# Moving one row per partition from the last block to the first: 113 and 15 rows in place of 112 and 16, in a streaming row maximum

## The chip, the cores and the metric

The kernel runs on one core of one Trainium2 chip. The metric is device time in microseconds (us), lower is better. It is taken as the median of several runs of the whole program; a profiled execution of the same program gives the trace that is read below.

## The reference

The computation is the maximum over the last axis of a float32 array:

```python
def setup_inputs():
    batch, seq, dim = 32, 512, 1024
    return {"x": np.random.randn(batch, seq, dim).astype(np.float32)}

def reference(x):
    return np.max(x, axis=-1).astype(np.float32)
```

That is 16,384 rows of 1,024 numbers, 67.1 MB in, 64 KB out. Every number is read once, so the work is one long stream of loads with a reduction behind it.

## The kernel before

**Tiling.** The rows are spread over 128 partitions, so each partition has 128 rows of 4 KB. A "row" below means one row in every partition: 128 x 1,024 numbers, 512 KB. The 128 rows form two blocks (`BLOCKS`, lines 13 to 16). In the first block partition p holds the 112 consecutive rows of x that begin at row 112 p, in the second the 16 consecutive rows that begin at row 14,336 + 16 p. So the distance in memory between the data of neighbouring partitions is 112 rows (448 KiB) in the first block and 16 rows (64 KiB) in the second.

**Loads.** Each entry of `BLOCKS` is one load, issued on the sync engine's queue (SP), line 238, in the order of the list: loads 0 to 10 for the first block, 11 to 17 for the second. The last two rows of the second block are not in the list: they come as four pieces of less than a row each (`PIECES`, line 243). The loads land in a ring of 47 row slots in the on-chip memory (`RING`). A load that doesn't fit before the end of the ring starts again at slot 0 (lines 112 and 113). Loads 0 to 3 take slots 0 to 46, loads 4 to 7 slots 0 to 41, and loads 8 to 17 and the pieces go round once more: load 10 (7 rows) is in slots 16 to 22, loads 11, 12 and 13 (3 rows each) in 23 to 31, load 14 (2 rows) in 32 and 33, loads 15, 16 and 17 (one row each) in 34 to 36, the pieces from 37 on. A load is issued when every earlier load whose slots it overwrites has been read (`issue`, lines 231 to 244).

**Reductions.** The vector engine (DVE) does nearly all of the maximum, with one instruction for each load: step `dJ` of `PLAN` (lines 31 to 34) is `direct(J)`, which reduces all rows of load J that are not shared. Every instruction of the body comes from the helper `maximum`, line 78.

**Shared rows.** Four of the late loads share some of their rows with other engines (`SHARED`, line 20; an entry is load: (rows, column blocks of 128)). `10: (3, 8)` says that three of load 10's seven rows go whole (all eight column blocks) to the other engines, so `d10` is left with four rows. `13: (2, 3)`, `14: (2, 3)` and `17: (1, 2)` say that of two rows, two rows and one row the first 3, 3 and 2 column blocks go to the other engines, and the rest of these rows, 640, 640 and 768 numbers wide, is reduced on DVE by the steps `p13`, `p14` and `p17` (`partial`). Load 13 has three rows, so one is left for `d13`; load 14 has two rows, both shared, so there is no `d14`.

The other engines' path is a step `tK` (`turn`): TensorE (PE) transposes each 128 x 128 block into PSUM, ScalarE (ACT) copies the result to a buffer, GpSimd (POOL) takes the maximum over the partitions. A step `bK` (`back`) then brings the row of maxima back into columns with small PE transposes. A chunk is at most as many rows as fit eight column blocks: `t0`, `t1`, `t2` are the three rows of load 10 (1,024 columns each), `t3` the two rows of load 13 (768 columns), `t4` those of load 14 (768), `t5` that of load 17 (256). `m10` (a DVE maximum over the 3 x 8 numbers that came back) closes load 10's rows, `m99` (over the 5 shared rows of loads 13, 14 and 17) closes the others and is the last reduction of the kernel.

**Order.** `PLAN` is the order of the steps, written out by hand, and the instructions of each engine are tied to it (`in_turn`). On DVE it gives d0 to d10, d11, d12, d13, p13, p14, m10, d15, d16, p17, then the four pieces f0 to f3, then m99. No instruction of DVE can overtake another that still waits for its load. `RANK` (line 22) puts the shared rows of loads 13, 14 and 17 at the end of the block's columns, so that `m99` writes neighbouring columns.

**Stores.** The first block's results are stored once f0 is done (line 265), the second block's after m99 (line 267), both on ACT's queue.

Of the kernel before, what the change touches and what calls it, by code (L numbers as in the profile page):

```python
# [10 lines left out]


BLOCKS = [
    [2, 15, 16, 14, 11, 11, 10, 10, 8, 8, 7],
    [3, 3, 3, 2, 1, 1, 1],
]
RING = 47


SHARED = {10: (3, 8), 13: (2, 3), 14: (2, 3), 17: (1, 2)}  # L20

RANK = {13: 1, 14: 2, 17: 2}

# [17 lines left out]
def kernel(  # L41
# [76 lines left out]
    assert first == I  # L118
    shared = [SHARED.get(j, (0, C)) for j in range(len(loads))]

# [176 lines left out]
```

## Time and profile before

| | |
|---|---|
| median of 3 runs | 163.84 us (163.82 to 163.93) |
| span of the profiled execution, first to last instruction | 162.1 us |
| instructions | 295 |
| DVE busy | 135.3 us, of it 129.9 us in reductions from the ring to the result |
| POOL busy | 15.9 us |
| PE busy | 13.6 us |
| ACT busy | 6.3 us |
| read from memory | 67.11 MB, mean 414 GB/s over the span |
| DVE's waits for loads | 23.5 us in four pieces: 3.14, 15.85, 3.20 and 1.30 us |
| last reduction (m99) | from 159.66 us, 0.17 us |
| last store issued | 159.86 us, lands 1.4 us later |

The span leaves out what lies before the first and after the last instruction: the median is 1.74 us longer than the span of the profiled execution. A difference between two kernels inside the span carries over to the median.

Times in the timeline are microseconds from the span's start. The duration of a DVE instruction overlaps the next one's start by some 0.08 us, because the instructions are pipelined; where instructions follow each other without a wait, the distance from start to start is therefore the cost, and it is a little less than the duration. A DMA's line gives the time from its issue to its landing, so the landing is the start of the issuing instruction plus that time.

### The profile page before, as it was taken

The page shows a single profiled execution, that of the slowest core. Times are in us where ns is not written, and L with a number is a line of the kernel's source. Part 1 is how long each engine was busy: PE and PEld are TensorE (multiplying, and loading weights), DVE is VectorE, ACT ScalarE, POOL GpSimd, SP SyncE. Part 2 cuts the span into 40 slices and gives each one's busy share as a digit, 9 for nine tenths or more (in the row PEclk, how much of TensorE's full clock was granted, in tenths as well). Part 3 has the DMA queues.
Part 4 walks back from the last instruction along what each step waited for, and adds up shares of the span by engine and source line. Part 5 has one row for each costly group of instructions (what it writes and reads, how often), then busy time and mean ns, then how long its engine had stood idle before and what let it go on. Part 6 is the DMA issues. An engine that isn't in the chain of part 4 may idle for free.

```text
span 162.1 us, 295 instructions
## 1 busy us (share of the span) xinstructions
PE 13.6 (8%) x76; PEld 11.7 (7%) x76; DVE 135.3 (83%) x33; ACT 6.3 (4%) x7; POOL 15.9 (10%) x10
## 2 busy tenths in 40 slices
PE   0000000000000000000000000000000000772942
PEld 0000000000000000000000000000000000762731
DVE  3500019998399999999999999996999999999994
ACT  3000000000000000000000000000000000241120
POOL 0000000000000000000000000000000000099791
PEclk9999999999999999999999999999999999996555
DMA  5995999599879999898999799799999989999991
GB/s 178 566 485 258 470 501 517 259 517 517 354 340 439 453 404 534 356 523 367 478 411 475 334 485 475 334 485 388 477 429 388 466 382 446 415 421 416 411 388 34
DMA packets 3456, 67.18 MB, mean 414 GB/s; under 512 B 640, under 2 KB 896, under 8 KB 1536
## 3 DMA queue, kind: packets, MB, share of 16 engines
q1 hardware_dynamic: 3168, 67.11, 96.8%
q10 hardware_dynamic: 288, 0.07, 0.2%
HBM read 67.11 MB, written 0.07 MB: 414 GB/s over the span
## 4 chain that ended last, share of the span: by engine, by line
DMA 50%; DVE 47%; SPq 1%; issue 0%; DVEq 0%
DMA ring<-in_x_dram 50%; DVE ring L78 45%; DVE joint L78 2%; SPq L238 1%; DVEq L292 0%
## 5 line engine op out<-in xcount | busy, mean ns | idle before, releaser
L78 DVE TENSOR_REDUCE ring<-ring 128x1 f32<-128x1024 f32 (+13 forms) x20 | 129.9, 6547 | 23.5 <-DMA ring<-in_x_dram 23.5
L168 POOL PARTITION_ALL_REDUCE top<-sb x6 | 15.7, 2658 | 142.6 <-ACT sb L166 142.5
L160 PE MATMUL ps<-ident,ring 128*128 128x128 f32 x38 | 9.0, 423 | 140.0 <-DMA ring<-in_x_dram 140.0
L160 PEld LDWEIGHTS ps<-ident,ring 128*128 128x128 f32 x38 | 7.6, 225 | 140.1 <-issue 140.1
L166 ACT COPY sb<-ps 128x1024 f32<-128x1024 f32 (+2 forms) x6 | 5.0, 834 | 150.5 <-PE ps L160 143.5
L78 DVE TENSOR_REDUCE joint<-ring 128x2 f32<-128x1280 f32 (+1 forms) x3 | 3.9, 1314 | 0.0
L178 PE MATMUL got<-ident,top 1*128 1x1 f32 x24 | 2.7, 228 | 3.8 <-POOL top L168 3.6
L178 PEld LDWEIGHTS got<-ident,top 1*128 1x128 f32 x24 | 2.4, 188 | 4.6 <-POOL top L168 4.6
L178 PE MATMUL joint<-ident,top 1*128 1x1 f32 x14 | 2.0, 244 | 1.9 <-POOL top L168 1.9
L178 PEld LDWEIGHTS joint<-ident,top 1*128 1x128 f32 x14 | 1.7, 210 | 2.7 <-POOL top L168 2.7
L166 ACT ACT_TABLE_LOAD x1 | 1.3, 1283 | 0.7 <-PEq L281 0.7
L83 DVE MEMSET ident<- 128x128 f32 x1 | 0.2, 165 | 0.8 <-PEq L281 0.8
L90 DVE TENSOR_SCALAR rowno<-rowno 32x1 f32<-32x1 f32 x3 | 0.4, 146 | 0.1
L85 DVE TENSOR_TENSOR_SCAN colno<-ident 128x128 f32<-128x128 f32 x1 | 0.4, 425 | 0.0
L92 DVE TENSOR_SCALAR ident<-colno,rowno 128x128 f32<-128x128 f32 x1 | 0.3, 288 | 0.0
L87 DVE STREAM_TRANSPOSE rowno<-colno 128x32 f32<-128x32 f32 x1 | 0.2, 211 | 0.0
L78 DVE TENSOR_REDUCE ring<-got 128x3 f32<-128x24 f32 x1 | 0.2, 172 | 0.0
L78 DVE TENSOR_REDUCE ring<-joint 128x5 f32<-128x20 f32 x1 | 0.2, 170 | 0.0
L281 POOL MEMSET const-float32-0.0<- 128x1 f32 x1 | 0.1, 98 | 0.2 <-issue 0.2
L281 POOL MEMSET const-bfloat16-1.0<- 128x1 bf16 x1 | 0.1, 102 | 0.0
L281 POOL MEMSET const-uint8-127<- 128x1 uint8 x1 | 0.1, 101 | 0.0
L281 POOL MEMSET const-float32-1.0<- 128x1 f32 x1 | 0.1, 98 | 0.0
(1 smaller groups left out, 0.1 us busy)
## 6 DMA issues: line engine op xcount, KB each, us to landing
ring<-in_x_dram SPq DMA_DIRECT2D x2, 5632.0 KB, 29.9
ring<-in_x_dram SPq DMA_DIRECT2D x2, 5120.0 KB, 36.8
ring<-in_x_dram SPq DMA_DIRECT2D x2, 4096.0 KB, 32.5
ring<-in_x_dram SPq DMA_DIRECT2D x1, 7680.0 KB, 22.6
ring<-in_x_dram SPq DMA_DIRECT2D x1, 7168.0 KB, 58.0
ring<-in_x_dram SPq DMA_DIRECT2D x3, 1536.0 KB, 35.7
ring<-in_x_dram SPq DMA_DIRECT2D x1, 3584.0 KB, 29.2
ring<-in_x_dram SPq DMA_DIRECT2D x2, 1024.0 KB, 17.8
```

The lines of the kernel that those rows point to most:

```text
L78: return in_turn("DVE", nc.vector.reduce_max(out=out, in_=in_, axis=X))
L83: in_turn("DVE", nc.vector.memset(ident, 1.0))
L85: in_turn("DVE", nc.vector.tensor_tensor_scan(out=colno, data0=ident, data1=ident, initial=-1.0, op0=ALU.add, op1=ALU.mult))
L87: in_turn("DVE", nc.vector.transpose(out=rowno, in_=colno[:, :32]))
L90: in_turn("DVE", nc.vector.tensor_scalar(out=part, in0=part, scalar1=float(q * 32), scalar2=None, op0=ALU.add))
L92: identity = in_turn("DVE", nc.vector.tensor_scalar(out=ident, in0=colno, scalar1=rowno[:, 0:1], scalar2=None, op0=ALU.is_equal))
L160: in_turn("PE", nc.tensor.transpose(out=ps[:, w:w + P], in_=rows(j)[:, lead[j] + r + i, c * P:(c + 1) * P], identity=ident,))
L166: in_turn("ACT", nc.scalar.copy(out=sb[:, :W], in_=ps[:, :W]))
L168: in_turn("POOL", nc.gpsimd.partition_all_reduce(top[:, :W], sb[:, :W], P, bass_isa.ReduceOp.max))
L178: in_turn("PE", nc.tensor.transpose(out=share(j)[:, r + i, c:c + 1], in_=tops[k][0:1, w:w + P], identity=ident[0:1, 0:1],))
L238: load = nc.sync.dma_start(out=rows(issued), in_=src)
L281: nc = _bacc.Bacc("TRN2", target_bir_lowering=False, num_devices=1)
```

## The change

```diff
 BLOCKS = [
-    [2, 15, 16, 14, 11, 11, 10, 10, 8, 8, 7],
-    [3, 3, 3, 2, 1, 1, 1],
+    [2, 15, 16, 14, 11, 11, 10, 10, 8, 8, 8],
+    [3, 3, 3, 1, 1, 1, 1],
 ]
 RING = 47
 
 
-SHARED = {10: (3, 8), 13: (2, 3), 14: (2, 3), 17: (1, 2)}
+SHARED = {10: (3, 8), 13: (2, 3), 14: (1, 3), 17: (1, 2)}
```

Load 10 has eight rows in place of seven, load 14 one row in place of two. The number of loads, the bytes, the ring and `PLAN` stay. What follows from the new numbers:

- `d10` reduces five rows in place of four; load 10 still shares three.
- `p14` reduces 640 columns of one row in place of two, and `t4` has 384 columns in place of 768 (three PE transposes, a smaller ACT copy and a smaller POOL maximum, three transposes back). `m99` takes four rows in place of five.
- Loads 11, 12 and 13 move up by one slot in the ring, to 24 to 32; load 14 is in slot 33, and the rest stays. Load 13 (slots 30 to 32) now overlaps slot 32, which belonged to load 7; before, load 14 was the first to overlap load 7.
- Partition p begins at row 113 p in the first block and at row 14,464 + 15 p in the second: the distance between neighbouring partitions becomes 452 KiB and 60 KiB. The stores write 452 and 60 bytes per partition in place of 448 and 64.

## The prediction

> **What bounds the kernel now.** I began with the page's busy times and DMA queues, which name two candidates: the loads (their packets fill 96.8% of the sixteen DMA engines' span) and DVE (busy 83%).
>
> ```profile
> PE 13.6 (8%) x76; PEld 11.7 (7%) x76; DVE 135.3 (83%) x33; ACT 6.3 (4%) x7; POOL 15.9 (10%) x10
> ...
> q1 hardware_dynamic: 3168, 67.11, 96.8%
> ```
>
> Shares over the whole span don't say which of the two ends last, so next I cut the span into windows. The columns are the window and its length, busy time of PE, its weight loads, DVE, ACT and POOL, the granted clock, the DMA share and GB/s.
>
> ```profile
> 60.00:75.00 15.00, 0.00 (x0) 0.00 (x0) 15.00 (x2) 0.00 (x0) 0.00 (x0) 1.00 1.00 433
> ...
> 121.00:139.00 18.00, 0.03 (x1) 0.06 (x1) 17.98 (x3) 0.00 (x0) 0.00 (x0) 1.00 1.01 432
> 139.00:150.00 11.00, 6.93 (x40) 6.42 (x40) 10.96 (x5) 3.04 (x3) 7.95 (x3) 0.89 1.00 422
> ```
>
> Both are full at once: the DMA share is 1.00 and DVE has no gap. Late in the kernel DVE sits exactly at the edge of the arriving data, and the question is who is ahead by how much at each load. For that I read two views side by side. The first is DVE's timeline (start, duration), one instruction a line; from d10 on they are d10, d11, d12, d13, p13, p14, m10, p17 and m99 (d15, d16 and the pieces are left out):
>
> ```profile
> 110.97 10.82 DVE L78 TENSOR_REDUCE ring<-ring 128x10 f32<-128x10240 f32 x1 [1.30 <-DMA ring<-in_x_dram]
> ...
> 139.00 4.41 DVE L78 TENSOR_REDUCE ring<-ring 128x4 f32<-128x4096 f32 x1
> 143.33 3.34 DVE L78 TENSOR_REDUCE ring<-ring 128x3 f32<-128x3072 f32 x1
> 146.59 3.34 DVE L78 TENSOR_REDUCE ring<-ring 128x3 f32<-128x3072 f32 x1
> 149.97 1.22 DVE L78 TENSOR_REDUCE ring<-ring 128x1 f32<-128x1024 f32 x1
> 151.11 1.49 DVE L78 TENSOR_REDUCE joint<-ring 128x2 f32<-128x1280 f32 x1
> 152.63 1.50 DVE L78 TENSOR_REDUCE joint<-ring 128x2 f32<-128x1280 f32 x1
> 154.03 0.17 DVE L78 TENSOR_REDUCE ring<-got 128x3 f32<-128x24 f32 x1
> ...
> 156.41 0.96 DVE L78 TENSOR_REDUCE joint<-ring 128x2 f32<-128x768 f32 x1
> ...
> 159.66 0.17 DVE L78 TENSOR_REDUCE ring<-joint 128x5 f32<-128x20 f32 x1
> ```
>
> The second is SP's timeline with the DMA issues of the same short windows (time to landing at the line's end). Here are loads 9, 10 and 14:
>
> ```profile
> 98.96 0.33 SPq L238 DMA_DIRECT2D ring<-in_x_dram  x1
> ring<-in_x_dram SPq DMA_DIRECT2D x1, 4096.0 KB, 31.4
> ...
> 109.69 0.33 SPq L238 DMA_DIRECT2D ring<-in_x_dram  x1
> ring<-in_x_dram SPq DMA_DIRECT2D x1, 3584.0 KB, 29.2
> ...
> 121.82 0.33 SPq L238 DMA_DIRECT2D ring<-in_x_dram  x1
> ring<-in_x_dram SPq DMA_DIRECT2D x1, 1024.0 KB, 30.6
> ```
>
> Load 9 lands at 98.96 + 31.4 = 130.36, load 10 at 109.69 + 29.2 = 138.89, load 14 at 152.42. In the same way load 7 lands at 110.97 (DVE's last long wait), loads 11 and 12 at 142.6 and 146.2. Load 13 is in the chain of waits:
>
> ```profile
> 111.01 38.94 DMA ring<-in_x_dram
> 149.95 0.02 issue
> 149.97 1.22 DVE ring L78
> ```
>
> It lands at 149.95. So at load 10 the loads are 0.11 us ahead of DVE (138.89 against 139.00), and at load 13 DVE is ahead by about 0.12 us: d12's step is 3.38 us from start to start, d11's, of the same size, 3.26. Behind it the loads are ahead: the last two pieces land at 158.47 and 158.97, and their reductions start at 158.57 and 159.14. From 139.00 to m99 at 159.66, then, DVE has one wait for data, of 0.12 us: **the last 20.7 us are DVE's**, and whatever delays DVE's start at d10 or adds to its work there moves the end.
>
> **The change, part by part.**
>
> *Load 10 lands later.* Its seven rows follow load 9 by 138.89 - 130.36 = 8.53 us, that is 1.22 us a row; the eight rows of load 9 took 9.7 us (load 8 landed at 87.17 + 33.5 = 120.67). Eight rows so land at 130.36 + 9.7 = 140.1; from 1.17 (9.70 - 8.53) to 1.22 us later than before. DVE is free at 139.00, since everything up to d9 is untouched, and can only wait. With a few hundredths for the pickup (load 9 was picked up 0.04 after its landing) d10 starts at 140.12: **+1.12 us**, bounds 1.06 to 1.22.
>
> *d10 has a fifth row.* From start to start one row takes 1.13 us, three 3.26, four 4.33, ten 10.73 (110.97 to 121.70): 1.07 a row more. **+1.07 us**.
>
> *p14 has half the work.* There is no row of 640 numbers into the joint tile. p14's 1.50 us for 1,280 numbers and p17's 0.96 for 768 give 0.00105 us a number with 0.15 fixed, so 640 cost 0.83 and 0.67 is saved; the plain pieces of 592 and 532 columns (0.758 and 0.697 us) give 0.81, and half of p14 would be 0.75. Bounds of the saving 0.53 (as dear as p17) to 0.75; I take **-0.65 us**.
>
> *The wait at d13 goes.* Load 13 lands one row later too, at about 151.15, but DVE reaches it at 140.12 + 5.40 + 2 x 3.26 = 152.04. **-0.12 us**. The 0.11 us by which p13's step (1.52) exceeds its work is a wait of p14 for p13's completion, and I leave it in.
>
> *What else moves, at no cost, with its cover.* Load 14 lands where it did: what is ahead of it and in it are as many rows as before. Everything behind it on SP's queue keeps its landing, and DVE comes 1.4 us later: d15, d16, p17 and the pieces find their data. Without that cover the price would be at most the row's difference, some 0.03 us a load by the one-row loads (1.28 a row against 1.22). In the ring, load 13 must now wait for d7, so it is issued at 121.8 in place of 111.0, and loads 14 and 15 behind it in SP's queue keep their time to within one issue, 0.4 us. At 121.8 the queue still holds loads 9 to 12, 22 rows, which last to 147.4: the cover is 25 us. The four pieces wait in SP's queue for loads 10 to 13 to land, so they are issued up to 1.2 us later; the last, issued at 151.2 in place of 150.0, has 7.8 us left to its turn.
>
> On the other engines t0 to t2 start 1.2 us later. POOL's three maxima (3.13, 3.21 and 3.30 us from 142.05) then end at about 152.9, and b2 at 153.9 (1.01 us of PE), before m10 is due at 155.4. t3 follows load 13: its POOL maximum from 153.8 to 156.3. t4's takes between 1.12 (256 columns) and 2.50 us (768), by interpolation 1.5. t5, behind b3 on PE, reaches POOL at 158.4 and ends at 159.5, and b5 at 160.0. m99 is due at 159.66 + 1.42 = 161.08: 1.1 us of cover.
>
> *The reads' pitch.* Neighbouring partitions lie 452 and 60 KiB apart, in place of 448 and 64. No row shows the new pitches. The nearest are the two old ones: loads 11 to 13 at 64 KiB take 11.06 us for nine rows (1.229), against 1.212 to 1.219 at 448 KiB for loads 8 to 10, and part of that is their size. So 1.4% at most, either way, taken over 139 us: 1.9 us as outer bounds. I take zero, because the engines are busy all the time at both pitches.
>
> The Trainium skill speaks against this zero: "DMA: Bandwidth & Descriptors", section "Latency and other measured facts", reports that copies slow down when the distance between partitions in memory is a large power of two (207 GB/s per direction at 512 KiB against 214 with 4 KiB of padding at 4 MiB, far less at 4 MiB without), and that 4 KiB more restores the rate; going from 448 to 452 KiB is just such a step. By that 3% the loads up to load 10 would be 4 us faster and the kernel faster than before, an estimate from that page; but 448 KiB is no power of two, and the trace's 433 GB/s leaves nothing of the kind to restore under the 435 GB/s that the same page, section "Where 436 GB/s comes from", gives as the ceiling.
>
> *The stores.* 60 bytes a partition in place of 64 at the end. The stores of 448 and 64 bytes land in 1.6 and 1.4 us, so I take no change, bounds 0.2 us either way.
>
> *Sum:* 1.12 + 1.07 - 0.65 - 0.12 = **+1.42 us**. The span goes from 162.1 to 163.5, and the median, 1.74 above the span, from 163.84 to 165.26; I say 165.25. The terms' bounds make it 1.06 + 1.07 - 0.75 - 0.12 = 1.26 to 1.22 + 1.07 - 0.53 - 0.12 = 1.64, so 165.1 to 165.5, and the stores widen it to 164.9 to 165.7.
>
> **The rivals.**
>
> *Faster reads (faster).* If the new pitch lets the loads through faster, load 10 lands earlier. To break even, it must be d10 that starts 0.30 us before 139.00 (end: +1.07 - 0.65 - 0.12 = +0.30): load 10 must land 1.42 us sooner than forecast out of 140.1, a gain of 1.0%. At 2% DVE's start at d2 moves by 0.86 us and the wait of 1.30 at d7 goes, load 10 lands at 137.3, and the time is 163.84 - 1.7 + 0.30 = 162.4 us. For it: DVE waits for data before d2 and d7, so it could use the gain. Against it: a DMA share of 1.00 with 432 to 433 GB/s in every long window. Chance 5%.
>
> *Slower reads (slower by more).* The same with the other sign: each 1% delays load 10 by 1.4 us, and all of it shows, 166.7 us. Chance 5%.
>
> *Cover by DVE's slack (no change).* If DVE had slack behind d10, the later start would be absorbed, as a gain upstream often is. The price would be what is left, 0 to 0.3 us, so 163.9. It needs 1.1 us of waits between 139.00 and 159.66, and the timeline shows 0.12. Chance 4%.
>
> *The other engines end last (slower).* If t5's path is late, m99 waits for it. It has 1.1 us of cover, so this decides from 1.1 us on; with POOL's maxima 0.6 us dearer each of the three late times, 165.9. Chance 2%.
>
> **How the numbers follow.** Forecast 84%, rivals 5, 5, 4 and 2. The predicted time is the forecast's, 165.25. Its own range 164.9 to 165.7 holds nearly all of its 84%; I take 164.7 to 165.8 for the runs' own scatter. A measurement of this kernel can tell about 0.2% (0.33 us) from no change. Slower is the forecast, the slower reads and the late engines, 91%; of the faster reads 5% are faster; 4% the same.
>
> **What would show it.** d10 at about 140.1 with a wait for a DMA of 1.1 us before it and a duration of 5.5; no wait between d12 and d13; p14 of 0.8 us; m99 at 161.1; load 7's landing unchanged at 110.97, which tests the pitch. It is wrong if d10 still starts near 139.0, if loads 1 to 9 land at other times than before, or if m99 waits for PE.

## The result and the profile after

The changed kernel takes 165.47 us (median of 4 runs, 165.3 to 165.5) against 163.88 us (163.82 to 163.99): a ratio of 1.0093, 95% interval 1.0081 to 1.0105. It is slower by 1.59 us. Beside later experiments, on one chip, the same two kernels gave 165.22 and 163.66, a ratio of 1.0090 (1.0076 to 1.0104), or 1.56 us. The profiled execution took 165.3 us with a span of 163.5, 1.4 more than the 162.1 of before.

The page's busy times and the loads' queue, of the kernel after:

```profile
PE 12.2 (7%) x70; PEld 10.4 (6%) x70; DVE 135.7 (83%) x33; ACT 6.0 (4%) x7; POOL 14.8 (9%) x10
...
q1 hardware_dynamic: 3168, 67.11, 96.1%
```

PE, ACT and POOL have less to do, DVE 0.4 us more, and the loads move the same bytes in the same number of packets. The totals would suggest 0.4 us; the kernel lost four times that. So the next view is the windows (same columns as before), where the shares of the stage show:

```profile
121.00:139.00 18.00, 0.00 (x0) 0.00 (x0) 17.92 (x3) 0.00 (x0) 0.00 (x0) 1.00 1.00 431
139.00:150.00 11.00, 5.96 (x36) 5.67 (x37) 10.04 (x3) 3.04 (x3) 6.89 (x3) 0.90 1.01 426
```

The loads run at the rate of before (431 against 432 GB/s). Between 139 and 150 us DVE is busy for 10.04 in place of 10.96 us: about one microsecond of idle time has appeared there. The DVE timeline says where. The lines are d7, then d10, d11, d13, p13 (which the view joins with p14), p14, m10, p17 and m99:

```profile
110.82 10.82 DVE L78 TENSOR_REDUCE ring<-ring 128x10 f32<-128x10240 f32 x1 [1.32 <-DMA ring<-in_x_dram]
...
139.96 5.49 DVE L78 TENSOR_REDUCE ring<-ring 128x5 f32<-128x5120 f32 x1 [1.03 <-DMA ring<-in_x_dram]
145.37 3.34 DVE L78 TENSOR_REDUCE ring<-ring 128x3 f32<-128x3072 f32 x1
...
151.88 1.21 DVE L78 TENSOR_REDUCE ring<-ring 128x1 f32<-128x1024 f32 x1
153.01 2.35 DVE L78 TENSOR_REDUCE joint<-ring 128x2 f32<-128x1280 f32 x2
154.53 0.83 DVE L78 TENSOR_REDUCE joint<-ring 128x1 f32<-128x640 f32 x1
155.26 0.17 DVE L78 TENSOR_REDUCE ring<-got 128x3 f32<-128x24 f32 x1
...
157.61 0.95 DVE L78 TENSOR_REDUCE joint<-ring 128x2 f32<-128x768 f32 x1
...
160.84 0.16 DVE L78 TENSOR_REDUCE ring<-joint 128x4 f32<-128x16 f32 x1
```

The reader is to see the bracket on d10: 1.03 us of waiting for a DMA, where the kernel before had none. Behind it no instruction waits for data.

SP's issue of load 10 and its landing, and the last store (issue to landing):

```profile
109.52 0.33 SPq L238 DMA_DIRECT2D ring<-in_x_dram  x1
ring<-in_x_dram SPq DMA_DIRECT2D x1, 4096.0 KB, 30.4
...
out_dram<-ring ACTq DMA_DIRECT2D x1, 7.5 KB, 1.6
```

Load 10 lands at 109.52 + 30.4 = 139.9, the moment at which d10 starts. The last store takes 1.6 us in place of the 1.4 of before:

```profile
out_dram<-ring ACTq DMA_DIRECT2D x1, 8.0 KB, 1.4
```

The whole stream begins at slightly different times in different executions: d0 starts at 5.65 us in the profile before, at 5.46 in this one and between 5.28 and 5.52 in the others below, and everything behind it moves along. So the sum is made from d7's start, the last long wait for a load that all the kernels share, to m99, and from m99 to the span's end:

| stretch | before | after | difference |
|---|---|---|---|
| d7 to d10 (load 10 lands later) | 28.03 | 29.14 | +1.11 |
| d10 to d11 (the fifth row) | 4.33 | 5.41 | +1.08 |
| d11 to d13 (the wait at d13) | 6.64 | 6.51 | -0.13 |
| d13 to p14 | 2.66 | 2.65 | -0.01 |
| p14 to m10 (half of p14) | 1.40 | 0.73 | -0.67 |
| m10 to m99 | 5.63 | 5.58 | -0.05 |
| d7 to m99 | 48.69 | 50.02 | **+1.33** |
| m99 to the span's end | 2.45 | 2.65 | **+0.20** |

The last row takes the span's end to the hundredth, 162.10 and 163.49 us, as the traces hold it. 1.33 + 0.20 = 1.53 us, close to the second pair of medians (1.56). The whole of the 0.20 us is the last store's landing. Its packets end 1.05 us after its issue in both traces; the 0.20 us lies between the last packet's end and the landing. In the two profiles the stream began 0.15 us earlier at d7 (110.82 against 110.97), which is why the spans differ by only 1.4.

### The profile page after: what moved, and what is told of

It reads as the page before. It is cut to its first block, busy times and chain, and to the rows that moved or that the text cites. A ratio compares the mean times of both kernels' runs of the same rounds, so it can differ in the third digit from the quotient of the medians.

```text
span 163.5 us, 282 instructions
## 1 busy us (share of the span) xinstructions
PE 12.2 (7%) x70; PEld 10.4 (6%) x70; DVE 135.7 (83%) x33; ACT 6.0 (4%) x7; POOL 14.8 (9%) x10
## 4 chain that ended last, share of the span: by engine, by line
DVE 52%; DMA 44%; issue 1%; SPq 0%; DVEq 0%
DVE ring L78 50%; DMA ring<-in_x_dram 44%; DVE joint L78 2%; SPq L238 0%; DVEq L292 0%
## 5 line engine op out<-in xcount | busy, mean ns | idle before, releaser
L168 POOL PARTITION_ALL_REDUCE top<-sb x6 | 14.6, 2481 | 144.2 <-ACT sb L166 144.2
L160 PE MATMUL ps<-ident,ring 128*128 128x128 f32 x35 | 8.0, 408 | 140.6 <-DMA ring<-in_x_dram 140.6
L160 PEld LDWEIGHTS ps<-ident,ring 128*128 128x128 f32 x35 | 6.6, 217 | 140.7 <-issue 140.6
L166 ACT COPY sb<-ps 128x1024 f32<-128x1024 f32 (+3 forms) x6 | 4.7, 781 | 151.4 <-PE ps L160 144.4
L78 DVE TENSOR_REDUCE joint<-ring 128x2 f32<-128x1280 f32 (+2 forms) x3 | 3.3, 1088 | 0.0
```

Source lines behind the costliest of these rows:

```text
L78: return in_turn("DVE", nc.vector.reduce_max(out=out, in_=in_, axis=X))
L160: in_turn("PE", nc.tensor.transpose(out=ps[:, w:w + P], in_=rows(j)[:, lead[j] + r + i, c * P:(c + 1) * P], identity=ident,))
L166: in_turn("ACT", nc.scalar.copy(out=sb[:, :W], in_=ps[:, :W]))
L168: in_turn("POOL", nc.gpsimd.partition_all_reduce(top[:, :W], sb[:, :W], P, bass_isa.ReduceOp.max))
```

## The experiments

Three theories were left to tell apart. *Sizes*: the time is lost on DVE, by the later landing of load 10 and the fifth row. *Pitch*: the other distance in memory between neighbouring partitions changes the reads. *Stores*: 60 bytes a partition land later than 64.

To part the division of the rows from the sizes of the loads, one edit takes the place of lines 99 to 117. It lets a list say which loads come from the second block, whatever their place in the order:

```diff
+SECOND = [11, 12, 13, 14, 16, 17]
...
-    for sizes in BLOCKS:
-        S = sum(sizes) + last * (sizes is BLOCKS[-1])
+    sizes = sum(BLOCKS, [])
+    column = {}
+    for mine in ([j for j in range(len(sizes)) if j not in SECOND], SECOND):
+        S = sum(sizes[j] for j in mine) + last * (mine is SECOND)
...
+        b = 0
+        for j in sorted(mine, key=lambda j: RANK.get(j, 0)):
+            column[j] = (xb[:, b:b + sizes[j], :], first + b)
+            b += sizes[j]
         first += S
+    for j, n in enumerate(sizes):
+        if at + n > RING:
+            at = 0
+        loads.append((at, n) + column[j])
+        at += n
```

**The division alone (e1_blocks_only).** The kernel before with this edit and the list above: sizes of before, 113 and 15 rows.

> The sizes of the loads and every instruction on DVE, PE, ACT, POOL and SP are those of the kernel before; only the division of the rows into 113 and 15 is the change's (load 15 is taken from the first block). Sizes theory (the change costs what DVE loses: a later load 10 and a fifth row in d10): m99 stays at 159.66 to within 0.1 and d10 starts at 139.0. With the stores theory added (60 bytes a partition land 0.2 to 0.4 us later than 64): 164.1 to 164.3 us; without it 163.9. Pitch theory (the new distance between partitions slows or quickens the reads): load 7's landing moves away from 110.97 by over 0.3 us, and the time from 163.9 by over 0.4.

Measured: 163.93 us against 163.83, ratio 1.0004 (0.9996 to 1.0013). Its DVE timeline (d0, d7, d10, m99), and its last store:

```profile
5.31 2.29 DVE L78 TENSOR_REDUCE ring<-ring 128x2 f32<-128x2048 f32 x1 [2.80 <-DMA ring<-in_x_dram]
110.63 10.82 DVE L78 TENSOR_REDUCE ring<-ring 128x10 f32<-128x10240 f32 x1 [1.30 <-DMA ring<-in_x_dram]
138.66 4.41 DVE L78 TENSOR_REDUCE ring<-ring 128x4 f32<-128x4096 f32 x1
159.33 0.17 DVE L78 TENSOR_REDUCE ring<-joint 128x5 f32<-128x20 f32 x1
...
out_dram<-ring ACTq DMA_DIRECT2D x1, 7.5 KB, 1.6
```

From d0 to d7, both started by a landing, are 105.32 us, as before (110.97 - 5.65 = 105.32): reads 452 KiB apart are as fast as reads 448 KiB apart, to a few hundredths. The absolute starts in the expectation (159.66, 139.0, 110.97) are all missed by 0.33 us, because the stream began that much earlier. Taken by the letter, load 7's landing so meets one half of the sign that the pitch theory named, while the time, the other half, stayed; but the kernel before itself, profiled again (c4 below), has d7 at 110.64, so an absolute start can't tell the two apart. From d7, d10 comes after 28.03 and m99 after 48.70 us, both as before. The pitch theory falls. The last store is the exception: 1.6 us, and 2.65 us from m99 to the span's end. In the runs' times this is near their scatter: the expected 164.1 to 164.3 isn't reached, and the interval neither shows nor excludes 0.2 us.

**The sizes alone (e2_sizes_only, c2_sizes_112_16).** The changed kernel with `SECOND = [10, 13, 14, 16, 17]`: 112 and 16 rows. It ran twice, the second time beside the changed kernel itself (c1_after_again).

> All sizes and instructions of the changed kernel, with the rows divided into 112 and 16 as before (loads 11, 12 and 15 come from the first block, load 10 from the second). Sizes theory: d10 starts at 140.0 to 140.1 after a wait of 1.0 to 1.1 us, m99 at 160.8 to 161.1, so 1.2 to 1.4 us over the kernel before: 165.1 to 165.3 us; with the stores theory the last store lands 1.4 us after its issue, as before, and the time is 0.2 to 0.4 under the changed kernel's 165.47. Pitch theory: near the kernel before, 163.9.

> The sizes of the changed kernel with the division into 112 and 16 rows, as in the earlier run of this kind. Sizes theory: 1.0 to 1.4 us over the kernel before, 164.9 to 165.2; the last store lands 1.4 us after its issue.

> The changed kernel once more, beside the next two on one chip. Stores theory (the last store of 60 bytes a partition lands later than one of 64): 0.2 to 0.4 us over the division into 112 and 16 with the same sizes, 165.2 to 165.5 us; m99 starts 50.0 us after d7, as in both earlier runs with these sizes. If the gap of 0.48 us between the two medians was the chip's and not the stores': the same time as the 112 and 16 division to within 0.1.

Measured: 164.99 us both times, ratios 1.0070 (1.0058 to 1.0082) and 1.0076 (1.0063 to 1.0089). The first one's d7, d10 and m99, and its last store:

```profile
110.66 10.82 DVE L78 TENSOR_REDUCE ring<-ring 128x10 f32<-128x10240 f32 x1 [1.30 <-DMA ring<-in_x_dram]
139.79 5.49 DVE L78 TENSOR_REDUCE ring<-ring 128x5 f32<-128x5120 f32 x1 [1.02 <-DMA ring<-in_x_dram]
160.67 0.16 DVE L78 TENSOR_REDUCE ring<-joint 128x4 f32<-128x16 f32 x1
...
out_dram<-ring ACTq DMA_DIRECT2D x1, 8.0 KB, 1.4
```

The wait of 1.02 us and 50.01 us from d7 to m99 are back, with the old division: by the trace the sizes cost 1.32 us (50.01 less 48.69). In the runs' times they cost 1.16 and 1.33 us, the first a little less than the expected 1.2 to 1.4. The last store lands after 1.4 us. The changed kernel ran at 165.22 us (165.16 to 165.29) beside the 164.99 (164.92 to 165.10) of the same sizes with 112 and 16: 0.23 us, without overlap of the single runs, which agrees with the 0.20 us of the store. The other 0.25 of the 0.48 us between the first two medians isn't the store's: the changed kernel itself ran 0.25 us faster in this later set than in the first one, and the kernel before 0.22. Whether that is the chip or the start of the stream isn't shown.

**The later landing alone (e3_row_apart).** The changed kernel with the eighth row as a load of its own:

```diff
-    [2, 15, 16, 14, 11, 11, 10, 10, 8, 8, 8],
+    [2, 15, 16, 14, 11, 11, 10, 10, 8, 8, 7, 1],
...
-SHARED = {10: (3, 8), 13: (2, 3), 14: (1, 3), 17: (1, 2)}
+SHARED = {10: (3, 8), 14: (2, 3), 15: (1, 3), 18: (1, 2)}
-RANK = {13: 1, 14: 2, 17: 2}
+RANK = {14: 1, 15: 2, 18: 2}
```

In `PLAN` a new `d11` follows `t2`, and the later loads' numbers rise by one.

> The changed kernel, with load 10's eighth row as a load of its own behind it (reduced on DVE right after d10, which has four rows again). Sizes theory: the wait before d10 goes (d10 at 138.9 to 139.0), the row still costs 1.13 us, p14 is 0.67 us cheaper, the wait at d13 stays away: m99 0.3 to 0.4 us after the 159.66 of the kernel before; with the later landing of the last store 164.4 to 164.6 us. If the wait is not the cost (DVE's row and the rest alone), the time stays near 165.5.

Measured: 164.63 us, ratio 1.0053 (1.0041 to 1.0065), 0.6 to 0.8 us less than the changed kernel. The lines are d10, the reduction of the old load 13's direct row, and p17's (now p18):

```profile
138.72 4.41 DVE L78 TENSOR_REDUCE ring<-ring 128x4 f32<-128x4096 f32 x1
...
150.99 1.22 DVE L78 TENSOR_REDUCE ring<-ring 128x1 f32<-128x1024 f32 x1 [0.21 <-DMA ring<-in_x_dram]
...
156.99 0.96 DVE L78 TENSOR_REDUCE joint<-ring 128x2 f32<-128x768 f32 x1 [0.19 <-PE joint L178]
```

d10 starts 28.03 us after d7 (110.69) again, so the wait is gone. Of its 1.1 us only part comes back: from d7 to m99 are 49.55 us, 0.47 less than in the changed kernel, where 0.9 to 1.0 was expected. Some 0.06 us of the rest is the price of reducing the row in an instruction of its own. Most went into two small waits further on, which DVE reaches because it is no longer late: for the load of three rows, which lands one row later than before (0.21 us idle, 0.30 from start to start: 3.56 in place of 3.26), and for PE, whose transposes `b3` write the same `joint` tile as this step (0.19 us idle, 0.27 from start to start). In the changed kernel the wait at d10 had covered both.

**The fifth row alone (e4_fifth_row).** The kernel before with `10: (2, 8)` in `SHARED`, and `t2` and its way back left out of `PLAN` (later chunks are renumbered).

> The kernel before, with two in place of three of load 10's rows shared, so that d10 has five rows and all loads stay as they were. Sizes theory: no wait before d10 (139.0), the fifth row adds 1.07, the wait of 0.12 at d13 goes: m99 at 160.6, 164.8 us. If DVE's work after d10 has slack behind it, as the rival of the prediction on no change says: 163.9. If the fifth row alone is the change's cost, with the wait hidden: as slow as the changed kernel, 165.5.

Measured: 164.49 us, ratio 1.0042 (1.0030 to 1.0054), 0.66 us more than before. The lines are d7, d10, d11 and m99:

```profile
110.69 10.82 DVE L78 TENSOR_REDUCE ring<-ring 128x10 f32<-128x10240 f32 x1 [1.30 <-DMA ring<-in_x_dram]
138.71 5.48 DVE L78 TENSOR_REDUCE ring<-ring 128x5 f32<-128x5120 f32 x1
144.10 3.34 DVE L78 TENSOR_REDUCE ring<-ring 128x3 f32<-128x3072 f32 x1
...
160.24 0.17 DVE L78 TENSOR_REDUCE ring<-joint 128x5 f32<-128x20 f32 x1
```

From d7 (110.69) to m99 (160.24) are 49.55 us: 0.86 more, where 0.95 was expected. The row itself costs 1.06 (5.39 us from d10 to d11, in place of 4.33), the wait at d13 goes (0.12), and a few hundredths of waits behind it go too. So DVE's work after d10 has no slack to speak of behind it; the rival of no change falls. The median of the runs shows 0.2 us less than the trace's 0.86, and 0.3 less than the 164.8 expected; that is within what the start of the stream differs between executions, but no run shows that this is the reason.

**What the store wants (c3_sizes_120_8, c4_before_again, s96, s56, s52, s48).** The list `SECOND` also gives other divisions: 120 and 8 rows with the sizes of the changed kernel, and 104 and 24, 114 and 14, 115 and 13, 116 and 12 with those of before; c4 is the kernel before once more.

> The sizes of the changed kernel with the rows divided into 120 and 8: stores of 480 and 32 bytes a partition, reads 480 and 32 KiB apart. If a store of whole multiples of 64 bytes a partition is what lands early: the last store lands after 1.6 us or more, as with 60 bytes, and the time is that of the changed kernel. If only a size that is no power of two lands late: 1.4 us, and the time of the 112 and 16 division. The sizes theory has m99 50.0 us after d7 in either case; the pitch theory has another landing of load 7.

> The kernel before, for a second profile: all theories expect 163.8 to 163.9 us, m99 48.7 us after d7, and a last store that lands 1.4 us after its issue. The first load's landing, which differs by up to 0.35 us between the profiles so far, moves everything behind it as a whole.

> Sizes of the kernel before, rows divided into 104 and 24: the last store has 96 bytes a partition. If a partition's share that is a multiple of 32 bytes lands early, as 32 and 64 do: 1.4 us. If only shares that never cross a 64-byte line do: 1.5 to 1.6. Sizes theory in either case: m99 48.7 us after d7; pitch theory: load 7's landing differs.

> Sizes of the kernel before, rows divided into 114 and 14: the last store has 56 bytes a partition, no multiple of 32 and across 64-byte lines. Both ideas on the store: 1.5 to 1.6 us. Sizes theory: m99 48.7 us after d7.

> Sizes of the kernel before, rows divided into 115 and 13: the last store has 52 bytes a partition, no multiple of 32 and across 64-byte lines. Both ideas on the store: 1.5 to 1.6 us. Sizes theory: m99 48.7 us after d7.

> Sizes of the kernel before, rows divided into 116 and 12: the last store has 48 bytes a partition, a multiple of 16 that crosses 64-byte lines. Both ideas on the store: 1.5 to 1.6 us; if 16 bytes are the grain that matters: 1.4. Sizes theory: m99 48.7 us after d7.

Measured, with the kernels above put beside them (the span's end is again taken to the hundredth from the traces):

| kernel | bytes a partition, last store | issue to landing, us | m99 to the span's end, us | d7 to m99, us |
|---|---|---|---|---|
| s96 | 96 | 1.4 | 2.47 | 48.69 |
| c4_before_again | 64 | 1.4 | 2.44 | 48.77 |
| e4_fifth_row | 64 | 1.4 | 2.44 | 49.55 |
| e2_sizes_only | 64 | 1.4 | 2.43 | 50.01 |
| c2_sizes_112_16 | 64 | 1.4 | 2.43 | 50.02 |
| e1_blocks_only | 60 | 1.6 | 2.65 | 48.70 |
| c1_after_again | 60 | 1.6 | 2.63 | 50.02 |
| e3_row_apart | 60 | 1.5 | 2.61 | 49.55 |
| s56 | 56 | 1.6 | 2.64 | 48.70 |
| s52 | 52 | 1.7 | 2.70 | 48.72 |
| s48 | 48 | 1.4 | 2.45 | 49.35 |
| c3_sizes_120_8 | 32 | 1.4 | 2.45 | 50.01 |

c3 took 165.02 us (ratio 1.0078, 1.0065 to 1.0092), the time of the 112 and 16 division; c4 took 163.63, a little under the expected 163.8, with a stream that began 0.33 us earlier at d7 than in the first profile. Shares of 32, 48, 64 and 96 bytes land after 1.4 us, shares of 52, 56 and 60 after 1.5 to 1.7. Neither of my two ideas fits 48 bytes; a grain of 16 bytes does, that is, shares that are whole multiples of 16 land early. It rests on one profile each for 32, 48, 52, 56 and 96. The number of bytes doesn't make the store of 60 bytes late: those of 96 and 64 bytes are larger and land sooner. But the length of a share isn't parted from its place. Where a share is no multiple of 16, most shares also begin at a place in memory that is none, and the results' first column on the chip lies at such a place too; which of these matters is open. The first block's store follows the rule only in part: shares of 416, 448, 464 and 480 bytes land after 1.6 us, but those of 452 and 460 after 1.6 to 1.7 and the one of 456, in a single profile, after 1.9.

One profile is outside the table's pattern: in s48 m99 comes 0.65 us late. There load 13 took 4.2 us behind load 12 where its three rows otherwise take 3.7 us, and d13 waited 0.58 us for it. Load 13 comes from the second block (48 KiB between partitions), but so does load 12 ahead of it, which took the usual 3.7 us. Whether the pitch of 48 KiB did it or that one execution, a single profile can't say; it stays open.

## Why the prediction was right

The chain it named is the one that was measured, and its terms hold one by one:

- Load 10 later: forecast 1.12 us, measured 1.11, with the wait in front of d10 in the trace.
- The fifth row: forecast 1.07, measured 1.08; alone, in e4, 1.06.
- Half of p14: forecast 0.65 saved, measured 0.67. Its duration was taken as 0.83 from a straight line through two other shapes, and is 0.83.
- The wait at d13: forecast 0.12 saved, measured 0.13.
- The pitch at no cost: shown by e1, whose loads land as before. The rule of the Trainium skill that spoke against it ("DMA: Bandwidth & Descriptors", section "Latency and other measured facts": 4 KiB more of row pitch restore the rate) names pitches of 512 KiB and more that are powers of two, in copies from memory to memory; no run here has such a pitch, and going from 448 to 452 KiB changed nothing (105.32 us from d0 to d7 at both).
- The ring: load 13 waits for d7 and is issued 11 us later (121.67 in place of 111.01), and lands at 121.67 + 29.4 = 151.1, as forecast. No DVE instruction after d10 waited for a load.
- The other engines' cover: `b5` was to end at 160.0, ended at 159.31 + 0.37 = 159.7, and m99 started 1.1 us later, the cover that was forecast. PE even waits for DVE now:

```profile
PE joint L178 <- DVE joint L78: 1.1, 1, 1.1
```

These are the transposes `b4`, which write the `joint` tile only after p17. It cost nothing.

One term was mis-sized. **The stores** were taken at no change, with 0.2 us as the bound; they cost 0.20, the bound itself. The nearest rows, 448 and 64 bytes a partition, differ from 60 in size, and the number of bytes isn't what matters; both are multiples of 16, and 60 is not. The other small error goes the opposite way: m99 came 1.33 us later from d7, not 1.42, since the stretch from m10 to m99, which the forecast took as unchanged, lost 0.05 us, and the terms themselves are off by a hundredth or two each. Together they make 1.53 for 1.42. So part of the closeness is luck: a cost that was left out and small savings that were left out lie on opposite sides.

A reserve in the working was thinner than it looked. e3 shows that the later landing is not worth its full 1.1 us: take it away and 0.57 us of other waits (0.30 and 0.27) come out from under it, so that only 0.47 us are won. The sum was right because the kernel has the wait, not because the terms are independent.

No version here beats the kernel before, and none was looked for beyond these edits: there the last piece lands at 158.97 us and is picked up at 159.14, so DVE and the loads end within 0.2 us of each other.

## What to carry to other kernels

Where a consumer keeps pace with a saturated stream of loads, moving rows from a late load to an earlier one can cost twice, as it did here: the consumer waits for the larger load, and then has its rows to do. Price both from the landing times and the consumer's own line, and count from a common event, such as the last wait that both kernels share, because the start of the stream moves by a few tenths between executions. A wait that is removed may only uncover the next one (e3): the gain is the difference to the next wait, not the length of the wait.

## What was not expected of the hardware

A last store of 60, 56 or 52 bytes a partition landed 0.1 to 0.3 us later than one of 32, 48, 64 or 96 bytes (1.5 to 1.7 against 1.4 us), although it moves fewer bytes than the latter two. The packets ended equally early in all of them, 1.04 to 1.06 us after the issue; why the landing comes later is not shown. The first load's pickup, on which all later times rest, varied from 5.28 to 5.65 us between executions; the kernel before alone had 5.65 and 5.34.
